# When a planner puts sums of weights in line: three weights ahead, with their high parts a step later, in a streaming-encoder trunk

## The chip, the core and the metric

The kernel runs on one core of one Trainium2 chip. The metric is device time in microseconds (us) of one execution. TensorE (PE) multiplies, VectorE (DVE) and ScalarE (ACT) work elementwise, GpSimd (POOL) mostly issues DMAs that accumulate, and SyncE (SP) issues the loads from HBM. Each engine takes its own instructions in program order and waits on semaphores for the others.

## The reference

512 tokens of 1024 features pass two layers. Each layer is: a half-step SwiGLU feed-forward (1024 to 2816 and back), a mixer, a second half-step feed-forward, and a gated per-layer embedding, each followed by a residual and a LayerNorm. The mixer is a chunked mLSTM in layer 0 and a chunked gMLP in layer 1.

```
def swiglu_ffn(x, w_gu, w_d):
    g, u = jnp.split(x @ w_gu, 2, axis=-1)
    return (jax.nn.silu(g) * u) @ w_d

for i in range(DEPTH):                       # DEPTH = 2
    x = layer_norm(DN_ALPHA * x + 0.5 * swiglu_ffn(x, ffn1_wgu[i], ffn1_wd[i]), ...)
    mix = mlstm_mixer(x, ...) if i % 2 == 0 else gmlp_mixer(x, ...)
    x = layer_norm(DN_ALPHA * x + mix, ...)
    x = layer_norm(DN_ALPHA * x + 0.5 * swiglu_ffn(x, ffn2_wgu[i], ffn2_wd[i]), ...)
    ple = jax.nn.sigmoid(x @ ple_wg[i] + ple_bg[i]) * (p[i] @ ple_wp[i])
    x = layer_norm(DN_ALPHA * x + ple, ...)
```

All of it is float32.

## The kernel before

**Products.** Every float32 operand is kept as two parts, a high part (rounded by an ACT copy, L277 for weights, L955 for hidden activations) and a low part (the rest: operand minus high part). A product is three matmuls, `mm3` (L388 to L392): high by high, high by low, low by high. The low part of a weight is made in one of two ways: a DVE subtraction (L286 at once, or L292 later), or ACT writes the negated operand (L283) and a POOL DMA adds the operand to it (L284).

**Products of sums.** Most of the feed-forwards' matrices are multiplied by a scheme with seven products in place of eight, on blocks that are first added and subtracted. For the up projections `up_forms` (L131) gives seven weights per pair of blocks: `a11`, `a12`, `s2`, `s1`, `s3`, `s4`, `a22`. Two of these, `s2` (L142, L143) and `s3` (L150, L151), need two DVE operations of 128x1024 on the loaded blocks, in place, before they can be split. For the down projections `forms` (L102) gives seven weights too; `t2` (L115, L116) and `t1` (L120, L121) are the sums there. The activations' side has sums of its own (`UpForms`, made in ten small `step`s during the first two chunks, and `Group.sums`, L939 to L943).

**Order.** A feed-forward (`ffn`, L1127) goes through its hidden blocks in six chunks of 2, 4, 4, 4, 4, 4. The first four blocks are "plain": an ordinary product each, for gate and up, so the first chunk and half of the second consist of plain steps (loop at L1196), and one pair of the second chunk and two pairs of each later chunk go by seven products each (`up_products`, L1146). The down product of the chunk before is spread between these steps (`group.product`, tile `gps`), and its results are added to the tokens by `residual` (L775, L777), which frees the PSUM banks. `UpPair.take` (L1099) empties the banks of the up products: ACT copies at L1103, DVE adds at L1106 and L1108; `gate` (L1114) is the Silu at L1117; `gated` (L1119) multiplies, and in the last chunk also splits the result (L395, L396). The last chunk's down product is an ordinary one (`down`, L803, tile `dps`) with four weights.

**The planner.** The class `Weights` holds a list `order` of all weights of the program. `fill` (L249) goes through it in order as far as tiles are free: "main" has four split tiles, "rows" two, some stages open "rowsx" or "extra". For each weight it calls `make` (for a sum this issues the two DVE operations), then the ACT copy of the high part and the low part. While `apart` is set, low parts by DVE are not issued there but put in `pending`, and `lows` (L305) issues them one product later; also, a weight whose load was issued less than two clock steps ago is not taken (L259). `form_ahead(3)` (L310), called at the end of each of the seven-product steps (L1168), looks at the next three weights of the order and calls `make` for those whose parts are there, so that only the splitting is left to `fill`. `take` (L325) gives the next ready weight to PE, and `release` returns a tile and calls `fill`. `W.clock` counts one per product of sums and two per plain step.

Before the change `form_ahead` is not called in the plain steps, so there `fill` itself calls `make` for a sum, and the copy of its high part is the next thing on ACT's queue.

**The end of a feed-forward.** After the last chunk `ffn` clears `apart`, calls `fill` (L1229) and goes to `down`. `ffn_ends` holds the place in the order at which `fill` stops during the last chunk (`limit`), behind the four weights of `down`. Their tiles are "rowsx", "rows", "main", "main" in the feed-forwards before a gated embedding (`ple`), where a further "rows" tile ahead of them holds the transposed embedding input, and "main", "rows", "rowsx", "rows" in the others.

Of the kernel before, what the change touches and what calls it, by code (L numbers as in the profile page):

```python
# [21 lines left out]
TB = SEQ // P  # L22
# [28 lines left out]
class Weights:  # L51
# [4 lines left out]
    def __init__(self, nc, raw_pool, split_pool):  # L56
        self.nc = nc
        self.pools, self.free = {"main": split_pool}, {"main": W_BUFS, "none": 0}
        self.raw_pools, self.raw_bufs = {"raw": raw_pool}, {"raw": RAW_BUFS}
        self.raw_free, self.raw_at, self.raw_tags = deque(range(RAW_BUFS)), {}, {}  # L60
        self.loads, self.left, self.raws = [], [], {}
        self.queues, self.held_raws = defaultdict(deque), defaultdict(deque)
        self.order, self.next_split, self.in_place, self.by_dma = [], 0, set(), set()
        self.ready, self.taken, self.held = deque(), deque(), []
        self.apart, self.pending, self.made, self.after, self.formed = False, deque(), {}, {}, set()
        self.boxes, self.rank, self.loaded_at, self.clock = [], {}, {}, 0
        self.limit = None

    def open(self, kind, pool, n):
        self.pools[kind], self.free[kind] = pool, n  # L70
# [31 lines left out]
    def forms(self, kind, b11, b12, b22, b21):  # L102

        vec = self.nc.vector

        def raw(b):
            return self.raws[b[0]][b[1]]

        def as_loaded(b):
            return lambda: (raw(b), (b[0],))

        def t2():
            vec.tensor_sub(raw(b12), raw(b22), raw(b12))  # L115
            vec.tensor_add(raw(b11), raw(b12), raw(b11))  # L116
            return raw(b11), ()

        def t1():
            vec.tensor_sub(raw(b21), raw(b21), raw(b11))  # L120
            vec.tensor_sub(raw(b11), raw(b22), raw(b11))  # L121
            return raw(b11), (b11[0],)

        made = [((b11[0],), as_loaded(b11)), ((b12[0], b22[0], b21[0]), as_loaded(b21)), ((), t2),
                ((), t1), ((), as_loaded(b12)), ((), as_loaded(b22)), ((), as_loaded(b21))]
        for _, make in made:
            self.in_place.add(make)
        self.after.update({t2: (made[0][1],), t1: (made[1][1], t2)})
        return [(kind, js, make) for js, make in made]

    def up_forms(self, j11, j12, j21, j22, by_dma=UP_BY_DMA):  # L131

        vec, raws = self.nc.vector, self.raws

        def a11():
            return raws[j11], ()

        def a12():
            return raws[j12], ()

        def s2():
            vec.tensor_add(raws[j21], raws[j21], raws[j22])  # L142
            vec.tensor_sub(raws[j11], raws[j21], raws[j11])  # L143
            return raws[j11], ()

        def s1():
            return raws[j21], (j21,)

        def s3():
            vec.tensor_sub(raws[j12], raws[j12], raws[j11])  # L150
            vec.tensor_sub(raws[j11], raws[j22], raws[j11])  # L151
            return raws[j11], (j11,)

        def s4():
            return raws[j12], (j12,)

        def a22():
            return raws[j22], (j22,)

        made = [((j11,), a11), ((j12,), a12), ((j21, j22), s2), ((), s1), ((), s3), ((), s4), ((), a22)]  # L160
        for _, make in made:
            self.in_place.add(make)
        self.after.update({s2: (a11,), s3: (a12, s2)})
        self.by_dma.update(made[r][1] for r in by_dma)
        return [("main", js, make) for js, make in made]

# [82 lines left out]
    def fill(self, most=1000, low=None, meanwhile=None):  # L249

        while most and self.next_split < len(self.order) and self.next_split != self.limit:
# [3 lines left out]
            for j in js or ():  # L255
                while j not in self.raws:
                    if not self.load(self.loads[j][1]):
                        return meanwhile
                if self.apart and self.ready and self.loaded_at[j] > self.clock - 2:  # L259
                    return meanwhile  # L260
            shape = [P, 2, 512]
            if js is not None:
                while any(m not in self.formed for m in self.after.get(make, ())):
# [61 lines left out]
    def take(self):  # L325
        tries = 0
        while not self.ready:
            assert tries < 10, (self.free, self.held_raws, self.next_split, self.held)
            tries += 1
            self.refill()  # L330
        self.kind, tiles = self.ready.popleft()
        while any(lo is tiles[1] for lo, _ in self.pending):
            self.lows(1)
        if not self.kind.startswith("rows"):
            self.taken.append(self.kind)
        return tiles
# [23 lines left out]
def hybrid_trunk(ctx: ExitStack, tc, x, p, ln_g, ln_b, ffn1_wgu, ffn1_wd, ffn2_wgu, ffn2_wd,  # L360
# [100 lines left out]
    def add_rows(w, kb, n, kind="main"):  # L461
        for k in range(0, n, 2):
            W.add((kp(w)[:, kb + k:kb + k + 2, :], rows2), kind=kinds_of(kind, k))
# [9 lines left out]
    LAST = len(FFN_CHUNKS) - 1  # L473
    PLAIN = 4
    AFFINE_AT = ((0, 1), (0, 2), (1, 0), (1, 1))
    turn_p, ffn_ends = [], []

    def plain_blocks(c):
# [6 lines left out]
    def ffn_weights(wgu, wd, name, ple=False):  # L485
# [35 lines left out]
                        W.order.append(down_w.popleft())  # L521
        if ple:
            W.add_hook("rows", lambda hi, lo: turn_p.pop()(hi, lo))
        add_rows(wd, starts[LAST], 4, ["rowsx", "rows", "main", "main"] if ple else ["main", "rows", "rowsx", "rows"])
        ffn_ends.append(len(W.order))


    ML_SLOTS = (2, 3, 4, 5, 6, 7, 11)
# [257 lines left out]
    def run_affine(n=1, by_dma=False):  # L786
        for _ in range(n):
            if affine:
                affine.pop(0)(by_dma)
# [13 lines left out]
    def down(hs, first, norm=None, lazy=False, defer=False):  # L803
# [18 lines left out]
        for t in range(TB):  # L822
# [26 lines left out]
            def finish(t=t, banks=banks):  # L849
                for half, ps in enumerate(banks):  # L850
                    residual(t, half, ps, first)
                    if norm is not None:
                        norm.stats(t, half, 2)
                if norm is not None and t == TB - 1:
                    norm.apply(t)
                    set_hooks(norm)

            if defer and t == TB - 1:
                return finish
            finish()  # L860
            if first:
                run_affine()

# [263 lines left out]
    def ffn(layer, k, rows, late, prepare=None):  # L1127
        with stage_pool("forms", 2) as fpool, stage_pool("quarters", Q_BUFS) as qpool, \
# [17 lines left out]
            def up_products(c, n, h, plain):  # L1146
                nonlocal norm
                steps = 7 * (n - plain) // 2
                for s in range(steps):
# [3 lines left out]
                    pair.product(r)  # L1153
                    W.clock += 1
                    group.add()
                    if r == 5 and h is None:
                        pair.parts = [W.spare(name).rearrange("p (b t) -> p b t", b=2) for _ in range(2)]
                        hs.extend([a[:, e] for a in pair.parts] for e in range(2))
# [26 lines left out]
            for c, n in enumerate(FFN_CHUNKS):  # L1185
# [4 lines left out]
                plain = plain_blocks(c)  # L1190
                if c == 0:
                    formed = UpForms(tpool, late)
                W.apart = not plain
                if c == LAST:
                    W.limit = ffn_ends.pop(0)
                for i in range(2 * plain):  # L1196
# [15 lines left out]
                        group.form()  # L1212
                    if (c, i) in AFFINE_AT:
                        run_affine(by_dma=True)
                    for _ in range(1 if (c, i) < (1, 2) else 2):
                        formed.step()
                if c == 0:
# [3 lines left out]
                else:  # L1221
# [3 lines left out]
                        next_group.form()  # L1225
                    group.add()
                    group = next_group
            W.apart, W.limit = False, None
            W.fill()  # L1229
            return down(hs, False, norm, lazy=layer == 0, defer=prepare is not None)  # L1230

    def ffn_stage(layer, k):
# [725 lines left out]
```

## Time and profile before

| what | value |
|---|---|
| median of 3 runs | 2229.39 us (2228.38 to 2229.95) |
| the profiled execution, its own time | 2231.84 us |
| its span, first to last instruction | 2230.1 us |
| PE busy | 2178.2 us (98%) |
| DVE busy | 1765.0 us (79%) |
| ACT busy | 1244.1 us (56%) |
| POOL busy | 254.3 us (11%) |
| mean granted PE clock | 0.989 |

Times inside the execution count from its first instruction. The lines name a line of the kernel, an engine, an operation and the tiles it writes and reads (`whi`, `wlo`: parts of a weight; `wbox`, `wquarter`, `wraw`: loaded weights; `ups`, `gps`, `dps`: PSUM tiles of the up products, the chunks' down products and the last down product; `us`: a copy of an up product; `fhi`, `flo`: parts of a hidden activation). The idle time that a line gives is that of the engine just before the instruction, with the instruction that let it go. An engine that waits for several others is put down to the one that came last. The granted clock is 1.00 or 0.50 of full speed for PE in any stretch. The first two of the four feed-forwards are those of layer 0: their second chunks lie around 60 to 90 us and 797 to 845 us; those of layer 1 around 1210 to 1260 us and 1838 to 1890 us.

### The profile page before, as it was taken

The page shows a single profiled execution, that of the slowest core. Times are in us where ns is not written, and L with a number is a line of the kernel's source. Part 1 is how long each engine was busy: PE and PEld are TensorE (multiplying, and loading weights), DVE is VectorE, ACT ScalarE, POOL GpSimd, SP SyncE. Part 2 cuts the span into 40 slices and gives each one's busy share as a digit, 9 for nine tenths or more (in the row PEclk, how much of TensorE's full clock was granted, in tenths as well). Part 3 has the DMA queues.
Part 4 walks back from the last instruction along what each step waited for, and adds up shares of the span by engine and source line. Part 5 has one row for each costly group of instructions (what it writes and reads, how often), then busy time and mean ns, then how long its engine had stood idle before and what let it go on. Part 6 is the DMA issues. An engine that isn't in the chain of part 4 may idle for free. (4 is left out here: it accounts for less than half of the span.)

```text
span 2230.1 us, 33273 instructions
## 1 busy us (share of the span) xinstructions
PE 2178.2 (98%) x13109; PEld 1944.7 (87%) x13109; DVE 1765.0 (79%) x2540; ACT 1244.1 (56%) x1712; POOL 254.3 (11%) x311
## 2 busy tenths in 40 slices
PE   9899999999999999999999899999999998999998
PEld 8899998888888888999888799998888887999987
DVE  6788887777776788888887788887788777888887
ACT  4666666464646536666455666665244455666632
POOL 1111100011101111111000111100011101111100
PEclk9999999999999999999999999999999999999999
DMA  6777764376747468777434787763348747777641
GB/s 211 166 189 191 181 155 127 89 160 133 161 113 151 113 170 189 185 194 171 151 115 136 171 196 185 180 159 126 123 83 157 176 124 169 192 183 185 141 151 57
DMA packets 232837, 346.29 MB, mean 155 GB/s; under 512 B 9780, under 2 KB 164532, under 8 KB 232680
## 3 DMA queue, kind: packets, MB, share of 16 engines
q0 software_dynamic: 56832, 117.64, 31.3%
q1 hardware_dynamic: 169232, 211.83, 29.2%
q10 hardware_dynamic: 6616, 14.69, 2.0%
q8 instruction: 103, 1.69, 0.3%
q14 instruction: 54, 0.44, 0.1%
HBM read 224.58 MB, written 2.11 MB: 102 GB/s over the span
## 5 line engine op out<-in xcount | busy, mean ns | idle before, releaser
L277 ACT ACTIVATE whi<-wbox 128x1024 fp32r<-128x1024 f32 x252 | 265.2, 1054 | 281.5 <-DVE wbox L143 117.6
L390 PE MATMUL ups<-xh,whi 128*128 128x256 f32 x1152 | 330.8, 287 | 23.5 <-ACT us L1103 23.5
L392 PE MATMUL ups<-xh,wlo 128*128 128x256 f32 x1152 | 330.4, 287 | 0.0
L391 PE MATMUL ups<-xl,whi 128*128 128x256 f32 x1152 | 330.3, 287 | 0.0
L390 PE MATMUL gps<-whi,fhi 128*128 128x512 f32 x644 | 253.1, 393 | 3.1 <-DVE xt L775 3.1
L391 PE MATMUL gps<-wlo,fhi 128*128 128x512 f32 x644 | 252.4, 392 | 0.0
L392 PE MATMUL gps<-whi,flo 128*128 128x512 f32 x644 | 251.5, 391 | 0.0
L277 ACT ACTIVATE whi<-wraw 128x1024 fp32r<-128x1024 f32 (+1 forms) x196 | 200.7, 1045 | 90.1 <-DVE wraw L121 22.6
L390 PEld LDWEIGHTS ups<-xh,whi 128*128 128x128 f32 x1152 | 225.5, 196 | 27.6 <-ACT us L1103 25.2
L284 POOL DMA_DIRECT2D wlo<-wbox x160 | 135.6, 847 | 950.9 <-ACT wlo L283 538.7
L391 PEld LDWEIGHTS ups<-xl,whi 128*128 128x128 f32 x1152 | 225.3, 196 | 2.4
L392 PEld LDWEIGHTS ups<-xh,wlo 128*128 128x128 f32 x1152 | 225.3, 196 | 0.0
L777 DVE TENSOR_TENSOR xt<-xt,gps 128x512 f32<-128x512 f32 x302 | 195.6, 681 | 29.2 <-PE gps L392 29.2
L286 DVE TENSOR_TENSOR wlo<-wraw,whi 128x1024 fp32r<-128x1024 f32 (+1 forms) x132 | 157.5, 1213 | 38.5 <-ACT whi L277 37.7
L277 ACT ACTIVATE whi<-wquarter 128x1024 fp32r<-128x1024 f32 (+1 forms) x140 | 135.2, 966 | 66.5 <-DVE wquarter L121 25.9
L283 ACT ACTIVATE wlo<-wbox 128x1024 fp32r<-128x1024 f32 x160 | 167.1, 1044 | 0.0
L392 PEld LDWEIGHTS gps<-whi,flo 128*128 128x128 f32 x644 | 121.0, 188 | 26.9
L390 PEld LDWEIGHTS gps<-whi,fhi 128*128 128x128 f32 x644 | 121.3, 188 | 25.7 <-ACT t_wlo L1039 3.7
L958 DVE TENSOR_TENSOR flo<-h,fhi 128x512 fp32r<-128x512 f32 (+1 forms) x140 | 88.6, 635 | 65.8 <-ACT fhi L955 65.7
L391 PEld LDWEIGHTS gps<-wlo,fhi 128*128 128x128 f32 x644 | 121.4, 188 | 21.3
L292 DVE TENSOR_TENSOR wlo<-wquarter,whi 128x1024 fp32r<-128x1024 f32 (+1 forms) x116 | 139.2, 1200 | 0.0
L955 ACT ACTIVATE fhi<-h 128x512 fp32r<-128x512 f32 (+1 forms) x140 | 80.3, 574 | 40.5 <-DVE h L1206 23.4
(367 smaller groups left out, 5810.2 us busy)
## 6 DMA issues: line engine op xcount, KB each, us to landing
wlo<-wbox POOLq DMA_DIRECT2D x160, 512.0 KB, 5.6
wbox<-in_ffn_wgu_dram SPq DMA_DIRECT2D x144, 512.0 KB, 4.5
wquarter<-in_ffn_wd_dram SPq DMA_DIRECT2D x64, 512.0 KB, 6.0
wraw<-in_ml_w_in_dram SPq DMA_DIRECT2D x24, 1024.0 KB, 5.8
wlo<-wraw POOLq DMA_DIRECT2D x48, 512.0 KB, 6.5
wraw<-in_gm_w_in_dram SPq DMA_DIRECT2D x15, 1024.0 KB, 5.8
wraw<-in_ffn_wgu_dram SPq DMA_DIRECT2D x17, 512.0 KB, 4.8
wraw<-in_ffn_wd_dram SPq DMA_DIRECT2D x8, 1024.0 KB, 5.0
```

Of the source, the lines that this page charges most:

```text
L277: self.nc.scalar.activation(hi[:, s], src[:, s], AF.Copy)
L283: self.nc.scalar.activation(lo[:, s], src[:, s], AF.Copy, scale=-1.0)
L284: self.nc.gpsimd.dma_start(lo[:, s], src[:, s], accum_op=OP.add)
L286: self.nc.vector.tensor_sub(lo[:, s], src[:, s], hi[:, s].bitcast(F32))
L292: self.nc.vector.tensor_sub(lo, src, hi.bitcast(F32))
L390: mm(ps, st[0], mv[0], start=start, stop=False, skip_group_check=more)
L391: mm(ps, st[0], mv[1], start=False, stop=False, skip_group_check=more)
L392: mm(ps, st[1], mv[0], start=False, stop=stop, skip_group_check=more)
L777: vec.tensor_add(dst, dst, ps)
L955: sca.activation(hi, src, AF.Copy)
L958: vec.tensor_sub(lo, src, hi.bitcast(F32))
```

## The change

- The planner gets a set `sums`, which holds the weights `t2`, `t1`, `s2` and `s3`, and a switch `ahead`, on from the second chunk of a feed-forward to its end. While it is on, `fill` stops at a sum that `form_ahead` has not made yet. Only when `take` finds nothing ready for the second time does it let `fill` make the sum itself (`forced`).
- `form_ahead(3)` is also called in each plain step, ahead of the small steps of `UpForms`.
- At a feed-forward's end `apart` stays set for the last `fill`, so the low parts made by it wait in `pending`. `down` issues them when a weight is taken, or one after each of the first two blocks of tokens and the rest after the third. In the last step of the last chunk (13) pending low parts are issued before the bank is emptied and the result gated, not after.
- Before a gated embedding the four weights of `down` take tiles "rowsx", "main", "rows", "main", and `limit` stands ahead of the fourth.

```diff
@@ Weights.__init__
-        self.limit = None
+        self.limit, self.ahead, self.forced, self.sums = None, False, False, set()
@@ forms
+        self.sums.update((t2, t1))
@@ up_forms
+        self.sums.update((s2, s3))
@@ fill
                 if self.apart and self.ready and self.loaded_at[j] > self.clock - 2:
                     return meanwhile
+            if self.ahead and not self.forced and make in self.sums and make not in self.made:
+                return meanwhile
@@ take
             tries += 1
+            self.forced = tries > 1
             self.refill()
+        self.forced = False
@@ ffn_weights
-        add_rows(wd, starts[LAST], 4, ["rowsx", "rows", "main", "main"] if ple else ["main", "rows", "rowsx", "rows"])
-        ffn_ends.append(len(W.order))
+        add_rows(wd, starts[LAST], 4, ["rowsx", "main", "rows", "main"] if ple else ["main", "rows", "rowsx", "rows"])
+        ffn_ends.append(len(W.order) - (1 if ple else 0))
@@ down
             finish()
+            W.lows(1 if t < TB - 2 else 100)
             if first:
                 run_affine()
@@ up_products                                    (DOWN_STEPS = 13)
                     group.add()
+                    if h is None and s == DOWN_STEPS:
+                        W.lows()
@@ ffn
-                W.apart = not plain
+                W.apart, W.ahead = not plain, c > 0
...
                     if (c, i) in AFFINE_AT:
                         run_affine(by_dma=True)
+                    W.form_ahead(3)
                     for _ in range(1 if (c, i) < (1, 2) else 2):
                         formed.step()
...
-            W.apart, W.limit = False, None
+            W.limit = None
             W.fill()
+            W.apart = W.ahead = False
             return down(hs, False, norm, lazy=layer == 0, defer=prepare is not None)
```

1 line of the change is left out of this document (added).

## The prediction

> **What bounds the kernel now.** I read the page's first part, then who TensorE (PE) waited for, then the stretches of low clock, then ScalarE's (ACT) and VectorE's (DVE) timelines around each wait. First the page:
>
> ```profile
> span 2230.1 us, 33273 instructions
> PE 2178.2 (98%) x13109; PEld 1944.7 (87%) x13109; DVE 1765.0 (79%) x2540; ACT 1244.1 (56%) x1712; POOL 254.3 (11%) x311
> ```
>
> PE is busy for 2178.2 of 2230.1 us, so nothing that leaves its matmuls alone can take away more than its idle time and what it loses to a low clock. The view of waits, for PE alone (total, times, longest):
>
> ```profile
> PE ups L390 <- ACT us L1103: 30.4, 8, 6.3
> PE dps L391 <- DVE wlo L292: 6.0, 2, 3.0
> PE gps L390 <- DVE xt L775: 3.1, 3, 1.1
> ...
> PE ups L391 <- DMA t_wlo<-x_f: 1.1, 4, 0.3
> ```
>
> These four are 40.6 us, and they come in fours and twos: once per feed-forward in its second chunk (8 waits are two in each of four), and once at the end of the two feed-forwards that a gated embedding follows. After most of them the clock falls. The view of windows gives busy time and count per engine, then the granted clock (0.50 or 1.00); below are two of the seven half-clock stretches (those behind the two ends), and the sum over the seven; then, from PE's timeline, two matmuls of the same product at full clock:
>
> ```profile
> 1097.33:1100.74 3.41, 3.41 (x10) 2.63 (x9) 3.41 (x4) 0.00 (x0) 0.00 (x0) 0.50 0.92 306
> ...
> 2138.40:2145.22 6.82, 5.91 (x14) 4.66 (x15) 5.39 (x5) 0.89 (x1) 0.00 (x0) 0.50 0.71 231
> sum 44.35, PE 34.12 PEld 32.10 DVE 26.30 ACT 24.89 POOL 6.31; mean PE 4.87 PEld 4.59 DVE 3.76 ACT 3.56 POOL 0.90
> ```
>
> ```profile
> 1091.60 0.40 PE L390 MATMUL dps<-whi,wquarter 128*128 128x512 f32 x1
> 1091.83 0.40 PE L391 MATMUL dps<-wlo,wquarter 128*128 128x512 f32 x1
> ```
>
> 14 matmuls in 5.91 us start 0.42 us apart, those two 0.23: so 0.45 of the 34.12 busy us at half clock is loss, 15.4 us. Ceiling of the whole change: 40.6 + 15.4 = 56.0 us.
>
> **Part one: the sums of the second chunk.** In the second chunk two blocks are plain and one pair is done by products of sums. Today `fill` calls `make` when it reaches a sum, so DVE gets two 1024-wide operations and ACT, next in program order, stands behind them with the high part. PE, ACT and DVE in the second of the four feed-forwards, from their timelines (start, duration, in brackets the idle time before and its releaser):
>
> ```profile
> 823.22 0.47 PE L390 MATMUL gps<-whi,fhi 128*128 128x512 f32 x1 [1.04 <-DVE xt L775]
> 826.81 0.38 PE L390 MATMUL ups<-t_whi,whi 128*128 128x256 f32 x1 [1.97 <-ACT us L1103]
> 827.49 0.44 PE L391 MATMUL ups<-t_wlo,whi 128*128 128x256 f32 x1 [0.29 <-DMA t_wlo<-x_f]
> 841.02 0.38 PE L390 MATMUL ups<-xh,whi 128*128 128x256 f32 x1 [4.80 <-ACT us L1103]
> ```
>
> ```profile
> 817.01 1.06 ACT L277 ACTIVATE whi<-wbox 128x1024 fp32r<-128x1024 f32 x1 [6.02 <-DVE wbox L143]
> 820.21 0.42 ACT L955 ACTIVATE fhi<-h 128x256 fp32r<-128x256 f32 x1 [2.15 <-DVE h L943]
> ...
> 826.19 0.57 ACT L1103 ACTIVATE us<-ups 128x512 f32<-128x512 f32 x1
> ...
> 834.20 1.07 ACT L277 ACTIVATE whi<-wbox 128x1024 fp32r<-128x1024 f32 x1 [6.50 <-DVE wbox L151]
> ...
> 839.05 0.61 ACT L1117 ACTIVATE us<-us 128x512 f32<-128x512 f32 x1
> ...
> 840.39 0.57 ACT L1103 ACTIVATE us<-ups 128x512 f32<-128x512 f32 x1
> ```
>
> ```profile
> 806.87 0.69 DVE L286 TENSOR_TENSOR wlo<-wquarter,whi 128x512 fp32r<-128x512 f32 x1 [0.76 <-ACT whi L277]
> 807.82 1.23 DVE L286 TENSOR_TENSOR wlo<-wbox,whi 128x1024 fp32r<-128x1024 f32 x1 [0.26 <-ACT whi L277]
> 810.01 0.43 DVE L958 TENSOR_TENSOR flo<-h,fhi 128x256 fp32r<-128x256 f32 x1 [0.97 <-ACT fhi L955]
> ...
> 815.75 1.22 DVE L143 TENSOR_TENSOR wbox<-wbox 128x1024 f32<-128x1024 f32 x1
> 818.10 1.23 DVE L286 TENSOR_TENSOR wlo<-wbox,whi 128x1024 fp32r<-128x1024 f32 x1 [1.12 <-ACT whi L277]
> ...
> 822.39 1.28 DVE L775 SCALAR_TENSOR_TENSOR xt<-xt,gps 128x512 f32<-128x512 f32 x2
> ...
> 826.01 0.69 DVE L286 TENSOR_TENSOR wlo<-wquarter,whi 128x512 fp32r<-128x512 f32 x1 [1.75 <-ACT whi L277]
> ...
> 831.69 1.22 DVE L150 TENSOR_TENSOR wbox<-wbox 128x1024 f32<-128x1024 f32 x1
> ...
> 834.09 0.68 DVE L1106 TENSOR_TENSOR us<-us,ups 128x512 f32<-128x512 f32 x1
> ```
>
> PE's waits of 1.97 and 4.80 end with the copies at 826.19 and 840.39, which empty a PSUM bank. Both copies are late only because ACT stood 6.02 us and 6.50 us behind L143 and L151. No work is short; the order is.
>
> After the change I replay the queues with these rows. By the planner's windows of three, the sum `t1` moves from plain step 1 to step 0, `s2` (L142, L143) from step 2 to the end of step 1, and `s3` (L150, L151) from the pair's first step to the end of plain step 2. The pair's quarters are the first four of six loads on SP's queue:
>
> ```profile
> 784.40 15.50 SPq L241 DMA_DIRECT2D wbox<-in_ffn_wgu_dram  x6
> ```
>
> They leave in the first chunk, over 20 us ahead of L143 at 815.75, so no age test and no DMA should hold the moved sums. The one DMA that `s3` must not overtake is that of `a12`'s low part, whose source L150 overwrites:
>
> ```profile
> wlo<-wbox POOLq DMA_DIRECT2D x160, 512.0 KB, 5.6
> ```
>
> It is issued in plain step 1, and between it and L150's new place stand five 1024-wide DVE operations of 1.2 us and several short ones: no wait. The count of instructions on each engine is unchanged.
>
> On DVE the waits 0.76, 0.26 and 0.97 go (ACT no longer waits for `t1` there) and the 1.12 goes (s2's high part is ready when s2's low part comes up): 3.11 us. ACT's next true wait, 820.21 for L943, shifts by these 3.11, and with it the copy: 823.08 instead of 826.19. But L150 and L151 now stand ahead of L775, 831.69 to 834.09 = 2.40 us; so L775 moves from 822.39 to 821.68, only 0.71 earlier. The three waits then become:
> - L775 frees the bank 0.71 earlier: 1.04 becomes 0.33.
> - PE comes to the next product 0.71 earlier, at 824.13 (826.81 - 1.97 - 0.71); the copy would let it go at 823.70. The wait is gone; what is late next is the low part by DMA, 827.49 - 3.11 = 824.38, so 0.25 stays.
> - ACT comes to s3's high part about 1.4 us after the copy, at 824.5 instead of 834.20, since the sum is then over. The copy at 840.39 would follow at 830.7 (6.19 us of ACT work lie between). The Silu before it (839.05, so 829.35) waits for L1106: 834.09 - 0.71 - 1.75 - 2.40 = 829.23, done at 829.91. The copy slips by 0.6 to 831.3, PE may start at 831.9. PE itself arrives at 831.6 (841.02 - 4.80 - 3.11, and 0.45 x 3.41 = 1.5 less with the clock up): 0.3 stays.
>
> Together 0.9 us a stage. A replay with every wait at its upper end (L1060 behind L1055, L943 0.2 later) gives 1.9. I take 1.2, nearer the rows: 4 x 1.2 = 4.8 us that stay. For gaps of a third of a us I count no clock. In the chunks after it the moved sums change nothing: the pointer of `fill` stands four weights ahead of PE there, and the existing call after each product has put every sum in line a step before `fill` reaches it; I find no sum that the new test would hold back. Cost of the test there: nothing, the cover being those four products.
>
> The moved sums stand on DVE closer to DMAs that the POOL queue issues. The view of the low parts' tile, durations as lowest/median/highest:
>
> ```profile
> L284 POOL DMA_DIRECT2D wlo<-wbox x160: 828/844/922, 54.6 to 2121.0; - x160
> ```
>
> 160 issues between 0.83 and 0.92 us, with DVE busy 79% of the time: no issue was held back. [...]
>
> **Part two: the feed-forwards' ends.** Around the end of the second feed-forward, PE, ACT and DVE:
>
> ```profile
> 1096.36 0.50 PE L391 MATMUL dps<-wlo,wquarter 128*128 128x512 f32 x1 [2.98 <-DVE wlo L292]
> ```
>
> ```profile
> 1088.98 2.95 ACT L277 ACTIVATE whi<-wraw 128x1024 fp32r<-128x1024 f32 x3 [1.45 <-PE gps L392]
> ...
> 1093.81 0.63 ACT L395 ACTIVATE wquarter<-us 128x512 fp32r<-128x512 f32 x1 [1.35 <-DVE us L1122]
> ```
>
> ```profile
> 1095.08 3.49 DVE L292 TENSOR_TENSOR wlo<-wraw,whi 128x1024 fp32r<-128x1024 f32 x3
> ```
>
> Weights two, three and four of the last product got their high parts together (x3) because weight two needed a "rows" tile that was still in use; their low parts came after the gating. Now weight two takes a "main" tile and is split a step earlier, weight three gets its low part before the gating, and the limit keeps weight four behind it. What is late next is weight four: high part after ACT's copy of 1093.81 (about 1094.6 to 1095.6), low part on DVE to 1096.9. PE starts the last product at 1091.60, as quoted, at 0.23 us a matmul; three weights are 18 of them, 4.14 us, and weight four's second one, at 1096.0, needs that low part: 0.9, say 1.0, stays of 2.98, twice: 2.0 us. Bounds: 0 (ACT frees itself sooner) and 2.98.
>
> **A cost.** `fill` at the end now runs with `apart` set, and refuses a load that is younger than two clock steps. Weight three of the mLSTM comes from a load issued one step before; weights one and two are still split there. ACT after the first feed-forward:
>
> ```profile
> 336.83 2.94 ACT L277 ACTIVATE whi<-wraw 128x1024 fp32r<-128x1024 f32 x3
> ...
> 363.14 0.63 ACT L650 ACTIVATE xh<-xf 128x512 fp32r<-128x512 f32 x1
> ...
> 365.88 1.50 ACT L647 ACTIVATE xf<-xps,cols 128x128 f32<-128x128 f32 x4 [2.10 <-PE xps L642]
> ```
>
> Of the three at 336.83 the third is put off until the mLSTM asks for it, and then four go in a row (3.9 us at 0.98) after 363.77, ahead of the transposed tokens at 365.88, which come at 367.7: 1.8 us later, and PE has little slack there. Bounds 0 and 3.9 us; I take 1.8. In the gMLP stage the last product of the feed-forward lets `fill` run again before the weight is needed: 0.
>
> **Sum.** 56.0 - 4.8 - 2.0 - 1.8 = 47.4 us. The profiled execution took 2231.84 us, 1.74 beyond its span and 2.45 over the median 2229.39 of the runs shown: 2184.4 profiled, 2182.0 as a median.
>
> After 2.98 us idle the clock stood at 0.50 in 2138.40:2145.22. The Trainium skill, "TensorE: Matmul & The Clock Gate", section "HAM oscillation — how this bites in real kernels", puts the limit at gaps over about 3.4 us; by that the two ends would lose no clock, and the sum would be 4.2 less (0.45 of 3.41 + 5.91), 2186.2. The row differs, and decides.
>
> **Rivals.** *DVE becomes the bound in the second chunk.* For it: L775, L1106 and everything behind them now stand after two sums. If the 3.11 us of DVE's waits do not come back, gps waits 1.04 + 2.40, the Silu some 1.5, and about 1.5 of clock is lost: 6.5 us a stage, 26 in all. Against it: those waits are plain rows. Time 2229.4 - (56.0 - 26 - 3.8) = 2203.2.
> *The sums are not put in line in the plain steps* (loads judged too young), so `fill` stops and the high part still stands behind them. Only the ends gain: 6.0 + 4.2 - 2.0 - 1.8 = 6.4, 2223.0. Against it: loads issued in the first chunk.
> *An issue by POOL is held back* behind the moved sums, by up to 2.4 us, and `s3`'s low part with it: 4 x 2.4 = 9.6 us, 2191.6. Against it: the 160 rows. [...]
> *Slower: weights come too late in chunks three to six.* If the new test holds `fill` until a product asks, PE waits for sum, high and low part, 2.4 + 1.06 + 1.23 = 4.7 us. There are 24 sums a feed-forward there, 96 in all; from eleven such waits on the 47.4 us are gone; with one sum in four it is 24 x 4.7 = 113 us, 2182 + 113 = 2295. Against it: the four-weight lead.
>
> **How the numbers follow.** Forecast 0.70, DVE-bound 0.20, not in line 0.04, late weights 0.04, held issue 0.02. 0.2% is 4.5 us, about what a measurement of this kernel can tell from no change. The range goes from the ceiling, 2229.4 - 56.0 = 2173.4, to the DVE-bound case, 2203.2 and a little over, 2205. Faster: 0.70 + 0.20 + most of the third case, 0.93; same 0.03; slower 0.04.
>
> **What would show it.** Right: PE's waits for L1103 fall from 30.4 to under 5 us, those on L292 from 6.0 to about 2; ACT's rows of L277 behind L143 and L151 lose their 6 us waits in the second chunks; the seven half-clock stretches go; a new wait of 1 to 2 us near 365 to 372. Wrong: PE waiting over 2 us a stage for L775; PE waits on whi or wlo in chunks three to six; half-clock stretches that stay.

## The result, and the profile after

The kernel after takes 2195.13 us (median of 5 runs, 2193.58 to 2196.67), the kernel before 2228.57 us (5 runs, 2226.66 to 2229.95): a ratio of 0.985, with a 95% interval of 0.9835 to 0.9864. Forecast were 2182.0 us, in a range from 2173.4 to 2205.0. The change wins 33.4 us between the medians, where 47.4 were forecast.

In the kernel after most lines have moved: PE's products are L396 to L398 (before L390 to L392), ScalarE's copy `us` is L1111 (L1103), its Silu L1125 (L1117), high parts L281 (L277), low parts on VectorE L290 and L296 (L286 and L292), the addition to `us` L1114 (L1106), the copies ahead of a low part by DMA L287 and GpSimd's issues L288 (L283 and L284).

The page's first part, after:

```profile
span 2191.9 us, 33268 instructions
PE 2167.9 (99%) x13109; PEld 1934.6 (88%) x13109; DVE 1761.8 (80%) x2540; ACT 1245.3 (57%) x1712; POOL 253.8 (12%) x311
```

The view of waits of PE, after (total, times, longest):

```profile
PE ups L396 <- ACT us L1111: 7.8, 4, 2.4
PE dps L397 <- DVE wlo L296: 1.5, 2, 0.8
PE warm L1923 <- POOL ident masks.py:199: 1.4, 1, 1.4
PE sup L888 <- ACT xh L657: 1.1, 2, 0.8
PE ups L398 <- DMA wlo<-wbox: 1.0, 2, 0.6
PE ups L397 <- DMA t_wlo<-x_f: 0.8, 3, 0.3
PE xps L649 <- DVE xt L764: 0.8, 2, 0.4
```

The copy's wait has fallen from 30.4 to 7.8 us, now one in each feed-forward instead of two; that on low parts at the ends from 6.0 to 1.5; that on the addition to x_t (3.1) is gone from the list. The 1.1 at L888 is the new wait at the mLSTM's start, the 0.8 at L649 a new one in the gated embeddings (two of 0.4).

The view of windows of the kernel after shows the half-clock stretches that are left (but for the one that the kernel's end cuts), each beginning within 0.8 us of the end of a wait of over 2 us (the window and its length, then PE, PEld, DVE, ACT and POOL busy, the granted clock, the DMA engines' share and GB/s):

```profile
827.22:830.63 3.41, 3.41 (x18) 3.41 (x17) 2.50 (x5) 2.85 (x4) 0.85 (x1) 0.50 1.02 202
1229.99:1233.40 3.41, 3.17 (x15) 3.17 (x16) 3.17 (x6) 3.41 (x5) 0.84 (x1) 0.50 1.10 237
1851.22:1854.63 3.41, 3.41 (x18) 3.41 (x17) 2.14 (x4) 2.48 (x4) 0.84 (x1) 0.50 1.02 211
```

At the prediction's 0.45 of PE's busy time, these 9.99 us cost 4.5 in this execution.

**The sum closes.** What was forecast to stay was 4.8 + 2.0 + 1.8 = 8.6 us. What stayed in the profiled execution: in the second chunks 7.8 + 1.0 + 0.8 of waits and 4.5 of clock; at the ends 1.5 + 0.8; at the mLSTM's start 1.1: 17.5 us. From the ceiling of 56.0 that leaves 38.5, and the two profiled executions differ by 2231.84 - 2193.58 = 38.3 us. The medians differ by only 33.4, because the profiled execution of before lay 3.3 us over its median and that of after 1.6 under its own.

**Where the missing 9 us are.** ScalarE's timeline in the second feed-forward, after:

```profile
815.88 0.58 ACT L1111 ACTIVATE us<-ups 128x512 f32<-128x512 f32 x1
...
817.30 1.05 ACT L281 ACTIVATE whi<-wbox 128x1024 fp32r<-128x1024 f32 x1
818.26 1.05 ACT L287 ACTIVATE wlo<-wbox 128x1024 fp32r<-128x1024 f32 x1
821.87 1.15 ACT L1068 ACTIVATE t_f<-x_d 128x512 fp32r<-128x512 f32 x2 [2.56 <-DVE xl L402]
...
824.82 0.61 ACT L1125 ACTIVATE us<-us 128x512 f32<-128x512 f32 x1
...
826.17 0.57 ACT L1111 ACTIVATE us<-ups 128x512 f32<-128x512 f32 x1
```

VectorE at the same place, after:

```profile
819.43 1.28 DVE L782 SCALAR_TENSOR_TENSOR xt<-xt,gps 128x512 f32<-128x512 f32 x2
820.62 1.22 DVE L402 TENSOR_TENSOR xl<-x_f,xh 128x1024 fp32r<-128x1024 f32 x1
821.76 0.68 DVE L1114 TENSOR_TENSOR us<-us,ups 128x512 f32<-128x512 f32 x1
```

The high part of the token quarter t4 (L1068, `t4_high` in `UpForms`) is written to the buffer that held t3 (both have the tag "f1"). VectorE still reads t3 for its low part (L402), which stands behind L782 and ends at 821.84. ScalarE waits 2.56 us for it, and the third product's copy `us` stands behind: PE, done with its other work at 824.40, goes on at 826.80. In the kernel before, ScalarE stood 6.50 us behind `s3` ahead of this copy, and t4's high part (there L1060) then had nothing to wait for. ScalarE's timeline, before:

```profile
836.12 1.13 ACT L1060 ACTIVATE t_f<-x_d 128x512 fp32r<-128x512 f32 x2
```

### The profile page after: what moved, and what is told of

Read it like the earlier page. It is cut to its first block, busy times and chain, and to the rows that moved or that the text cites. A ratio compares the mean times of both kernels' runs of the same rounds, so it can differ in the third digit from the quotient of the medians.

```text
span 2191.9 us, 33268 instructions
## 1 busy us (share of the span) xinstructions
PE 2167.9 (99%) x13109; PEld 1934.6 (88%) x13109; DVE 1761.8 (80%) x2540; ACT 1245.3 (57%) x1712; POOL 253.8 (12%) x311
## 5 line engine op out<-in xcount | busy, mean ns | idle before, releaser
L281 ACT ACTIVATE whi<-wbox 128x1024 fp32r<-128x1024 f32 x252 | 265.1, 1054 | 233.2 <-DVE wbox L144 99.9
L396 PE MATMUL ups<-xh,whi 128*128 128x256 f32 x1152 | 328.3, 285 | 7.8 <-ACT us L1111 7.8
L398 PE MATMUL ups<-xh,wlo 128*128 128x256 f32 x1152 | 328.1, 285 | 0.7 <-DMA wlo<-wbox 0.6
L396 PE MATMUL gps<-whi,fhi 128*128 128x512 f32 x644 | 253.0, 393 | 0.1
L281 ACT ACTIVATE whi<-wraw 128x1024 fp32r<-128x1024 f32 (+1 forms) x196 | 200.5, 1045 | 92.0 <-DVE wraw L121 22.6
L398 PE MATMUL gps<-whi,flo 128*128 128x512 f32 x644 | 251.5, 391 | 0.0
L288 POOL DMA_DIRECT2D wlo<-wbox x160 | 135.6, 848 | 920.7 <-ACT wlo L287 502.9
L396 PEld LDWEIGHTS ups<-xh,whi 128*128 128x128 f32 x1152 | 222.8, 193 | 11.9 <-ACT us L1111 9.5
L398 PEld LDWEIGHTS ups<-xh,wlo 128*128 128x128 f32 x1152 | 222.8, 193 | 1.1 <-DMA wlo<-wbox 1.1
L290 DVE TENSOR_TENSOR wlo<-wraw,whi 128x1024 fp32r<-128x1024 f32 (+1 forms) x124 | 148.1, 1213 | 39.7 <-ACT whi L281 38.9
L281 ACT ACTIVATE whi<-wquarter 128x1024 fp32r<-128x1024 f32 (+1 forms) x140 | 135.2, 966 | 59.2 <-ACT wlo L287 20.4
L287 ACT ACTIVATE wlo<-wbox 128x1024 fp32r<-128x1024 f32 x160 | 167.1, 1044 | 0.0
L398 PEld LDWEIGHTS gps<-whi,flo 128*128 128x128 f32 x644 | 120.9, 188 | 26.9
L396 PEld LDWEIGHTS gps<-whi,fhi 128*128 128x128 f32 x644 | 121.3, 188 | 22.3 <-issue 0.2
L296 DVE TENSOR_TENSOR wlo<-wquarter,whi 128x1024 fp32r<-128x1024 f32 (+1 forms) x116 | 139.2, 1200 | 0.0
```

The lines of the kernel that those rows point to most:

```text
L281: self.nc.scalar.activation(hi[:, s], src[:, s], AF.Copy)
L287: self.nc.scalar.activation(lo[:, s], src[:, s], AF.Copy, scale=-1.0)
L288: self.nc.gpsimd.dma_start(lo[:, s], src[:, s], accum_op=OP.add)
L290: self.nc.vector.tensor_sub(lo[:, s], src[:, s], hi[:, s].bitcast(F32))
L296: self.nc.vector.tensor_sub(lo, src, hi.bitcast(F32))
L396: mm(ps, st[0], mv[0], start=start, stop=False, skip_group_check=more)
```

## The experiments

What is disputed is what holds PE in the second chunk now. Theory: ScalarE at L1068. Rivals: VectorE as the engine that is full there (the prediction's own second case), or the low parts made by DMA. Ratios are to the kernel before, in runs beside it on the same chip. Its median was 2227.2 to 2228.57 us in these groups of runs, so a difference of medians from two groups is uncertain by about 1 us.

**The two parts of the change.** `sums_only` has the call of `form_ahead` in the plain steps, `ahead` and the stop, and leaves out the ends' edits:

```diff
-        add_rows(wd, starts[LAST], 4, ["rowsx", "main", "rows", "main"] if ple else ...
-        ffn_ends.append(len(W.order) - (1 if ple else 0))
+        add_rows(wd, starts[LAST], 4, ["rowsx", "rows", "main", "main"] if ple else ...
+        ffn_ends.append(len(W.order))
...
-            W.lows(1 if t < TB - 2 else 100)
...
-                    if h is None and s == DOWN_STEPS:
-                        W.lows()
...
+            W.apart = W.ahead = False
             W.limit = None
             W.fill()
-            W.apart = W.ahead = False
```

`ends_only` is the reverse:

```diff
-                W.apart, W.ahead = not plain, c > 0
+                W.apart, W.ahead = not plain, False
...
-                    W.form_ahead(3)
                     for _ in range(1 if (c, i) < (1, 2) else 2):
```

> The change's first part alone: sums put in line in the second chunk's plain steps, none of the edits at the feed-forwards' ends. Theory (the parts don't meet): the two waits at the ends come back (2.98 instead of 0.76 + 0.38, twice 1.84) with their half-clock stretches (0.45 of 3.41 and of 5.91 busy us, 4.2), and 1.07 us at the mLSTM's start go: 6.8 us more than the kernel after, about 2202. Rival: the ends' edits win nothing that lasts (what is won there is given back in the gated embedding, whose start then waits for VectorE): 2194 to 2197, as the kernel after.

> The change's second part alone: the order, the limit, the low parts and the last fill at the feed-forwards' ends, with sums formed in the second chunk as before the change. Theory: 6.8 us less than the kernel before, about 2221.8, with PE's waits on low parts (L292 of before) falling from 6.0 to about 1.5 us, and those of the second chunk unchanged at about 34 us. Rival: as before, 2227 to 2230, if what is won at the ends is given back in the gated embedding.

`sums_only` took 2200.28 us (ratio 0.9869, 0.9855 to 0.9882), `ends_only` 2225.88 (0.9988, 0.9979 to 0.9997). The sums win 28.0 us, the ends 2.4, together 30.4; both at once win 33.4. The waits at the ends and on the copy are as the theories have them in both. `sums_only` has one wait more than its theory: 5.6 us on low parts made by DMA, where the kernel after has 1.0 (see "The clock's share"). Its waits of PE:

```profile
PE ups L396 <- ACT us L1110: 7.6, 4, 2.4
PE dps L397 <- DVE wlo L296: 6.0, 2, 3.0
PE ups L398 <- DMA wlo<-wbox: 5.6, 6, 2.7
```

`ends_only`, waits of PE:

```profile
PE ups L396 <- ACT us L1111: 29.2, 8, 6.3
PE gps L396 <- DVE xt L782: 3.4, 3, 1.3
PE dps L397 <- DVE wlo L296: 1.5, 2, 0.8
```

The ends alone won 2.4 us instead of 6.8. Their waits fell as expected; its profiled span (2223.4) is 6.7 below that of before, and 4.3 of this is not in the medians. The clock's share of the forecast came from one execution of before that was 3.3 us slower than its median.

**The stop alone**: `sums_only` without the call in the plain steps.

```diff
-                    W.form_ahead(3)
                     for _ in range(1 if (c, i) < (1, 2) else 2):
```

> The change's stop alone: from the second chunk on a fill ends in front of a sum that isn't formed yet, but the plain steps put none in line, and the ends are as before the change. Theory: a sum of the second chunk then waits until PE has used every weight ahead of it; each of its sums costs VectorE's two 1.22 us, ScalarE's high part and the low part in the open, 3 to 6 us for each of some 3 in 4 stages, with the clock: 2260 (2235 to 2320), slower than before the change. Rival: the stop is what wins, since ScalarE no longer stands behind VectorE: 2200 to 2215.

2261.61 us (1.0151, 1.0133 to 1.017): slower, as expected. Its waits of PE:

```profile
PE ups L398 <- DMA wlo<-wbox: 25.2, 11, 5.3
PE ups L396 <- ACT whi L281: 19.4, 8, 4.6
```

This is the mechanism of the prediction's slower rival, in the second chunk. With `form_ahead` in the plain steps the stop never acts: leaving it out of the change gives the same list of instructions on all five engines.

**t4's high part a step later.**

```diff
-            self.last = {0: lambda: split(*self.t3, b), 1: t4_high, 2: t4_low}
+            self.last = {0: lambda: split(*self.t3, b), 2: t4_high, 3: t4_low}
```

> The kernel after, with ScalarE's high part of t4 (L1068) issued one step later, behind the copy us (L1111) of the third product, and VectorE's low part one step later too. Theory one: what is left of the third wait (2.40, 2.38, 2.22 and 0.79 us) is ScalarE standing 2.56 us at L1068 for VectorE's xl (L402), which reads the tile that L1068 writes. Then the waits on L1111 fall from 7.8 to under 1.5 us, the three half-clock stretches of 3.41 us go (3 x 1.5), and the time falls by 9 to 12 us, to about 2184.5. Theory two: VectorE is the bound there, and the copy stands behind Silu (L1125), which waits for VectorE's sum L1114; then L1068's own 1.15 us at most is won in each stage, the stretches stay, and the time falls by 0 to 4 us, to 2191 to 2195.

`t4_and_end` has this too, and the old last fill for feed-forwards without a gated embedding:

```diff
             W.limit = None
+            W.apart = prepare is not None
             W.fill()
```

> As the kernel with t4's high part a step later, and the last fill of the feed-forwards without a gated embedding is run with low parts in line again (apart off), as before the change. Theory: the 1.07 us at the mLSTM's start (0.23 at 360.97 and 0.84 at 363.02) come from that fill and fall to under 0.3; the ends of the two feed-forwards before the gated embedding keep their 0.76. So some 0.8 us less than with t4's step alone: about 2183.7, which the medians can hardly tell from it; the profile can. Rival: the four high parts in a row were needed, the low parts now stand ahead on VectorE, and a wait of about 1 us comes back elsewhere at those ends: no less than with t4's step alone.

They took 2197.09 (0.9851, 0.9836 to 0.9866) and 2195.97 us (0.9854, 0.9841 to 0.9868): no gain over the change itself. My theory was right on the copy and wrong on the time, and `t4_step_later` lies outside the ranges of both theories. `t4_and_end`, waits of PE:

```profile
PE ups L398 <- DMA wlo<-wbox: 13.6, 8, 3.1
PE dps L397 <- DVE wlo L296: 1.5, 2, 0.8
```

The waits on L1111 and the 1.1 at the mLSTM's start are gone from it. A wait on low parts made by DMA stands in their place, larger than the one removed, and the half-clock stretches did not go (granted clock 0.996, as in the kernel after). GpSimd's issues of them in `t4_and_end`, from its timeline:

```profile
819.64 0.86 POOL L288 DMA_DIRECT2D wlo<-wbox  x1 [3.32 <-ACT wlo L287]
821.53 0.84 POOL L288 DMA_DIRECT2D wlo<-wbox  x1 [1.04 <-ACT wlo L287]
827.69 0.85 POOL L288 DMA_DIRECT2D wlo<-wbox  x1 [5.31 <-ACT wlo L287]
```

PE's products that wait for them, the fifth, sixth and seventh of the pair:

```profile
826.46 0.39 PE L398 MATMUL ups<-xh,wlo 128*128 128x256 f32 x1 [1.44 <-DMA wlo<-wbox]
...
830.51 0.39 PE L398 MATMUL ups<-xh,wlo 128*128 128x256 f32 x1 [0.93 <-DMA wlo<-wbox]
...
835.81 0.38 PE L398 MATMUL ups<-t_f,wlo 128*128 128x256 f32 x1 [0.78 <-DMA wlo<-wbox]
```

From the issue to the product that waits for it that is 6.8, 9.0 and 8.1 us. The issues themselves take 0.84 to 0.86 us, like the others of that kernel (0.83 to 0.92); it is the transfers that are slow. The view of DMA traffic of the same kernel from 820 to 838 us (packets, MB, share of 16 engines; then KB each and the median us to landing):

```profile
q0 software_dynamic: 521, 1.94, 54.3%
q1 hardware_dynamic: 2014, 2.44, 43.5%
...
wlo<-wbox POOLq DMA_DIRECT2D x4, 512.0 KB, 8.4
```

The low parts (q0) and the weights' loads (q1) fill the sixteen engines to 98%. The Trainium skill, "DMA: Bandwidth & Descriptors", section "Anatomy of one DMA — SWDGE (gpsimd) path", fits a DMA issued from GpSimd by 2.0 us + bytes / 436e3, an estimate of 3.2 us for 512 KB; the rows differ, and decide.

**Low parts on VectorE.** In the second chunk the low parts of the fifth, sixth and seventh product's weights are made by VectorE, one, two or three of them. In the numbers of the code these are 4, 5 and 6, and `UP_BY_DMA` is (1, 3, 4, 5, 6):

```diff
-                                            by_dma=UP_BY_DMA if b == starts[c] + plain else ...
+                                            by_dma=(1, 3) if c == 1 else UP_BY_DMA if b == starts[c] + plain else ...
```

That is `low456_vec`; `low4_vec` has (1, 3, 5, 6) in this place. The kernels named `t4_low...` have both edits of `t4_and_end` as well, with (1, 3, 5, 6) for the fifth alone, (1, 3, 5) for the fifth and seventh, (1, 3, 6) for the fifth and sixth, and (1, 3) for all three.

> The kernel with t4's high part a step later and the old last fill, and in the second chunk the low part of the fifth product's weight (the one that PE waits for at 826.46) is made by VectorE (one 128x1024 subtraction, 1.22 us) instead of ScalarE's copy and a transfer on GpSimd's queue. Theory one: what replaced the wait on the copy is GpSimd's queue of transfers, one at a time (there they start at 824.52, 829.12, 832.96 and 837.63, 3 to 4.2 us each, while PE uses one weight in 3.75 us); with one transfer fewer the sixth's starts 4.6 us earlier, and PE's waits on wlo (13.6 us, 8 times) fall under 4 us, the half-clock stretches there go, and the time falls to 2184 to 2188. Theory two: the DMA engines as a whole are full there (their share 1.03 to 1.07 from 826 to 842), and SyncE's loads hold the low parts back whatever the queue: the sixth's and seventh's low parts land where they did, PE waits for them longer instead, and the time stays within 2 us of 2196.

> As the kernel before in this call, with the seventh product's low part in the second chunk made by VectorE too. Theory one: the seventh's transfer was due at the edge (landing 837.5, used at about 835.6); without it no wait on wlo is left in the second chunk, 1 to 3 us less than with the fifth alone, 2182 to 2186. Rival: VectorE (1.22 us more, with the x_t additions and the low parts of the downs behind it) is now last, and PE waits for gps or flo: 0 to 4 us more than with the fifth alone.

> The kernel after with only the second chunk's fifth low part moved to VectorE; t4's high part stays where it was. Theory: ScalarE's copy us (L1111), behind the high part of t4, is still last, so PE's waits on it stay at 7 to 8 us and the time at 2194 to 2197. Rival: the transfers were already the wait, and ScalarE's copy merely ended with them: 2188 to 2192.

> The kernel with t4 a step later and the old last fill, the fifth and the sixth product's low parts in the second chunk made by VectorE. Theory: GpSimd's queue carried the sixth's low part late (waits of 2.01 and 0.46 us with the fifth alone on VectorE); without it those go, PE's waits on wlo fall from 4.3 to under 1.5 us, and the time to 2183 to 2185. Rival: VectorE, with 2.4 us more in the second chunk, is late with a low part or with the additions to x_t: 2186 to 2189.

> As the kernel before in this call, with the seventh product's low part on VectorE too (3.7 us more there than in the kernel after, less ScalarE's 3 copies). Theory: nothing is left to gain, since the seventh's transfer has room once two are gone from the queue: within 1.5 us of the kernel before. Rival: VectorE becomes the bound of the second chunk at last: 2 to 6 us more.

> The kernel after, with the low parts of the fifth, sixth and seventh product's weights in the second chunk made by VectorE, and t4's high part where the change left it. Theory: two limits stand one behind the other, ScalarE's stand at t4's high part and GpSimd's queue of three transfers, and only without both does the time fall to 2178. Here the first stays, shorter by the sixth's copy (1.04 us) that no longer stands ahead of the copy us on ScalarE: waits on L1111 of 1.2 to 1.4 us in three stages, none on wlo<-wbox, no or one half-clock stretch, 2184 to 2187. Rival one: the transfers alone were the limit, and ScalarE's stand would have been covered: no waits on L1111, 2177 to 2180. Rival two: the waits on L1111 stay at 2.4 us in each stage, with their stretches: 2188 to 2192.

| low parts on VectorE | t4's high part where the change left it | t4 a step later, old last fill |
|---|---|---|
| none | 2195.13 (after) | 2195.97 |
| 5th | 2191.63 (0.9838, 0.9824 to 0.9851) | 2186.22 (0.9818, 0.9804 to 0.9831) |
| 5th, 7th | - | 2185.40 (0.9808, 0.9795 to 0.9822) |
| 5th, 6th | - | 2186.41 (0.9816, 0.9802 to 0.9831) |
| all three | 2183.30 (0.9795, 0.9781 to 0.9808) | 2177.78 (0.9775, 0.976 to 0.9789) |

With t4 a step later the fifth alone does nearly what theory one has it do: 4.3 us of waits on low parts are left of 13.6 (forecast were under 4), and 2186.22 us. Without that edit (`low4_vec`) it leaves the copy's wait where it was, as expected (8.0 us), but the time is 3.5 us lower and lies in the rival's range. The intervals of the two ratios overlap, though the runs do not (2191.09 to 2192.70 us against 2193.58 to 2196.67). The granted clock doesn't explain it: at 0.998 three runs of `low4_vec` took 2191.09 to 2191.93 us, and three of after 2194.62 to 2195.35. That the transfers make the difference, as the rival has it, fits with the table under "The clock's share", but no profile of after at that clock shows it.

The two limits stand one behind the other. Without the first alone nothing is won, without the second alone 11.8 us, without both 17.4 (some 1 us of it by the old last fill); against the kernel before in the same groups of runs, 10.6 and 16.0. In `t4_low456_vec` PE's waits are those that have nothing to do with the second chunk, but for 0.8:

```profile
PE dps L397 <- DVE wlo L296: 1.5, 2, 0.8
PE warm L1924 <- POOL ident masks.py:199: 1.4, 1, 1.4
PE xps L649 <- DVE xt L764: 0.8, 2, 0.4
PE ups L397 <- DMA t_wlo<-x_f: 0.8, 3, 0.3
```

`low456_vec` keeps ScalarE's stand at L1068; one copy (L287, 1.04) fewer stands behind it, and the wait is 0.9 us shorter, nearly as expected (1.4 to 1.5 us a stage, forecast 1.2 to 1.4; the time lies 0.7 us below its range). Its waits of PE:

```profile
PE ups L396 <- ACT us L1111: 4.4, 3, 1.5
```

VectorE as the bound is refuted. The same stretch in the view of windows, first after, then `t4_low456_vec` (the window and its length, PE, PEld, DVE, ACT, POOL busy, clock, DMA share, GB/s):

```profile
811.00:839.00 28.00, 25.25 (x177) 23.63 (x176) 22.76 (x33) 22.01 (x30) 5.09 (x6) 0.94 0.86 201
```

```profile
811.00:839.00 28.00, 27.66 (x202) 25.76 (x201) 27.41 (x38) 18.57 (x27) 2.56 (x3) 1.00 0.70 181
```

VectorE is busy for 27.41 of 28.0 us there, the DMA share has fallen from 0.86 to 0.70, and PE is not held. There is no more room on VectorE, though.

Besides `low4_vec`, three of these expectations failed. `t4_low46_vec` was to leave no wait on low parts; it left 5.7 us, more than with the fifth alone, so its time in the forecast range is luck. (The "edge" of its theory set a landing in `t4_step_later`'s execution beside a use in `t4_and_end`'s.) `t4_low45_vec` was to leave under 1.5 us of waits on the seventh's low part, alone in the queue; it left 5.5, and its time lies in the rival's range. GpSimd issues it at 825.15 there, and PE goes on at 831.59 (the timelines of GpSimd and PE in `t4_low45_vec`):

```profile
825.15 0.86 POOL L288 DMA_DIRECT2D wlo<-wbox  x1 [11.36 <-PE ups L398]
```

```profile
831.59 0.39 PE L398 MATMUL ups<-t_f,wlo 128*128 128x256 f32 x1 [1.45 <-DMA wlo<-wbox]
```

6.4 us for a single one: a queue of three is not the whole of it. Taking out the seventh as well (`t4_low456_vec`) won 8.6 us, where I had expected none. In the kernel after, such a transfer took 4.5 us at least and 6.0 in the median (the low parts' tile, all products); VectorE's own low part takes 1.22.

How much of it is the queue, and how much the loads beside it, no run separates by itself, but the DMA packets in the traces tell a part. In the kernel after, the low part issued at 815.44 has no load beside it: its first packet starts at 816.86, 1.4 us after the issue, and the last ends 2.8 us later. In `t4_low45_vec`, beside the loads, the seventh's first packet starts only at 827.95, 2.8 us after the issue, and the last ends 3.0 us later. In `t4_and_end` the sixth's first packet starts at 827.11, 5.6 us after the issue and behind the fifth's last, which ended at 826.10; the seventh's packets, beside the loads, take 4.6 us. This fits with both the queue and the loads adding to it; how much each is worth stays open.

**The clock's share.** 18 matmuls on old operands fill PE's wait on the copy, in the three feed-forwards where it is over 2 us; what they compute is used by nobody:

```diff
+                    if plain and s == 4 and (layer, k) != (0, 0):
+                        idle, a = up_bank("idle"), formed.right[0][0]
+                        for _ in range(18):
+                            mm(idle[:, :256], a[:, 0, :P], a[:, 0], start=True, stop=True)
                     pair.product(r)
```

> The kernel after, with 18 matmuls of 128x256 on old operands put on PE ahead of the fifth product of the second chunk, in the last three feed-forwards; their result is used by nobody. They start 0.11 to 0.12 us apart (the products' own), some 2.1 us in each wait of 2.40, 2.38 and 2.22 us on the copy us (L1111), so they lengthen nothing. Theory: the three half-clock stretches of 3.41 us follow from PE's idleness there; they go, and with them 0.45 of some 10 busy us, so the time falls by 4 to 5 us, to 2190.5 to 2191.5, with the copy as late as before. Rival: the clock falls for another reason (the load of the chip there): the stretches stay and the time stays at 2194 to 2197.

2196.03 us (0.9857, 0.984 to 0.9873). The stretches go, as the theory has it (granted clock 0.999 over the span of the profiled execution, after 0.996), and the time doesn't follow. Its waits of PE:

```profile
PE ups L398 <- DMA wlo<-wbox: 6.2, 7, 1.8
...
PE ups L396 <- ACT us L1111: 1.3, 3, 0.8
```

1.0 us of waiting for these low parts has become 6.2. That fits with PE coming, at half clock, late enough to the next products for their transfers; at full clock it waits. So in the kernel after, the 2.4 us on ScalarE and the slow matmuls behind them covered the transfers: removing either alone brings the transfers out.

The four kernels that leave t4's high part in place and form the sums ahead agree on this, stage by stage. PE's waits on these low parts in the second chunks, in us, with the half-clock stretches that lie there:

| kernel | 1st feed-forward | 2nd | 3rd | 4th |
|---|---|---|---|---|
| `after` | 1.0 | none, half clock | none, half clock | none, half clock |
| `sums_only` | 1.5 | 1.1 | none, half clock | 3.0 |
| `low4_vec` | 0.3 | 0.5 | 0.5 | none, half clock |
| `wait_filled` | 1.5 | 1.4 | 1.5 | 1.8 |

No stage with a stretch waits for one of these low parts, and every stage without one does. The stretch of `sums_only`, from the view of windows (that of `low4_vec` is in the last section):

```profile
1233.60:1237.01 3.41, 3.41 (x17) 3.41 (x18) 2.75 (x5) 3.09 (x4) 0.84 (x1) 0.50 1.05 216
```

The 4.5 us that the sum books for the clock are therefore no loss that could be had back by itself.

## Why the prediction was right, and what it sized wrongly

- **The second chunk's order was the cause**: shown. The sums alone win 28.0 of the 33.4 us, with the same count of products, and the stop, which never acts, has no part in it.
- **The first two waits**, in the second feed-forward: 1.04 was to become 0.33 (a gap of 0.07 is left), and 0.25 was to stay on the low part by DMA (0.28). Both right.
- **The step that was mis-sized is the third wait**: "The copy at 840.39 would follow at 830.7 (6.19 us of ACT work lie between)", and "0.3 stays". The start was right: s3's high part 1.4 us behind the copy (817.30 - 815.88 = 1.42), and PE 8.5 us behind it (824.40 - 815.88 = 8.52). But from that high part to the next copy lie 826.17 - 817.30 = 8.87 us: the 6.19 of work, and 2.56 of standing at L1068. I had taken the distance between ScalarE's rows over from before, without asking what each waits for once the longer wait in front of it is gone. 0.3 became 2.2 to 2.4 in three stages and 0.8 in the first.
- **"For gaps of a third of a us I count no clock"** fell with it: in the profiled execution the waits of over 2 us took 4.5 us of clock. So two of the prediction's signs failed: waits on the copy under 5 us (7.8), and no half-clock stretches left (three).
- **The ends**: 1.0 was to stay at each; 0.76 stayed, and 0.4 came up in the gated embedding, where low parts now stand on VectorE ahead of the tokens that PE transposes (`ends_only` has this wait, `sums_only` has not). By the prediction's terms ("Only the ends gain") they were to win 6.4 alone; they won 2.4 in the medians.
- **The mLSTM's start**: 1.8 us, because a load is judged too young; 1.1 measured, and gone with the old last fill, as the cause given says.
- **Rivals**: VectorE as the bound was refuted by the kernel that gave it 3.7 us more per second chunk. GpSimd's issues were not held back (0.84 to 0.86 us each); their transfers were what comes next, which no case of mine had. Late weights in chunks three to six did not come.
- **The total** came out in the range, with 33.4 us for 47.4, because the terms that were mis-sized are small beside the waits that went. The transfers, which the prediction did not have, did not come on top of the low clock: the two replace each other (the table above).
- **The base**: the sum against the profiled execution was right within 9.2 us, 2193.58 for 2184.4. Taking 2.45 us off for a median left 13.1, since both executions lie off their medians.

## What to carry to other kernels

When a wait goes, ask of each instruction behind it on the same engine what it waits for itself, shared buffers too; adding up durations finds only the work. Then go on to the next limit, a transfer's time from issue to landing above all: here ScalarE's wait hid the transfers, and two edits that alone win nothing and 11.8 us win 17.4 together, while filling PE's wait won nothing. Taking away a low clock behind a wait gains nothing by itself where what comes next is a transfer that lands no earlier for it.

## What the runs showed of the hardware

- Half-clock stretches came in lengths of 3.41, 6.83 or 10.24 us, and their starts lay whole multiples of 3.413 us apart within an execution (after: 1229.99 - 827.22 = 402.77 = 118 x 3.413; 1851.22 - 1229.99 = 621.23 = 182 x 3.413). Waits of the same length draw a stretch or none: of three waits of 2.2 to 2.4 us all three drew one in the kernel after, and of three of 2.4 us only one in `low4_vec`. A clock term read from one execution is so uncertain by a stretch or two, 1.5 us each.

`low4_vec`, waits of PE, and the one stretch:

```profile
PE ups L396 <- ACT us L1111: 8.0, 4, 2.4
```

```profile
1848.25:1851.66 3.41, 3.41 (x18) 3.41 (x18) 2.40 (x4) 2.74 (x4) 0.84 (x1) 0.50 0.70 130
```

- The Trainium skill, "TensorE: Matmul & The Clock Gate", section "HAM oscillation — how this bites in real kernels", has the clock fall after gaps of over about 3.4 us. Here 2.22 to 2.40 us of idleness were enough in the kernel after, though not each time (2.4 us twice in `low4_vec` drew none), while in the kernel with filled waits, where none was over 1.8 us, no stretch came. The rows decide.
